# A seven-product up projection in half of a layer's feed-forward part (fp32 split in two, one core)

## Chip, core and metric

One core of a Trainium2 chip runs the whole layer in one launch. The metric is the device time of one execution in microseconds (us); the kernel before has a median of 679.17 us over three runs (679.04 to 679.43).

## The reference

One decoder layer for 512 tokens of width 1024 in fp32: an attention part (a gated delta rule on four heads and block attention on four), a feed-forward part and a gated embedding. The change touches the feed-forward part alone:

```
u2 = rms_norm(h, mlp_pre_norm)                       # 512 x 1024
f  = square(relu(u2 @ w_up)) @ w_down                # w_up 1024 x 4096, w_down 4096 x 1024
h  = h + rms_norm(f, mlp_post_norm)
h  = h + sigmoid(h @ w_ple_gate) * (p @ w_ple)
```

## The kernel before

Every large matmul is done in fp32 by three passes: each operand is split into a high part (a cast to fp32r, on ScalarE) and a low part (the rest, a subtraction on VectorE), and `mm3` (L194) multiplies high by high, high by low and low by high. So each operand tile costs one cast and one subtraction, in `split` (L773) or written out at L958 and L959.

The hidden width 4096 is 32 blocks of 128 columns. Blocks q and q + 16 form pair q; the 16 pairs stand in five groups of 3, 4, 4, 4 and 1 (`GROUPS`, L809). The output of a pair is a tile of `F`, two sides of 512 tokens each. `up` (L881) computes one side: it loads a block of w_up (512 KB), splits it, and runs 8 x 3 matmuls of 512 columns against the normalised, transposed input `u2T`, which is kept split; then ScalarE takes relu and, after the second side, the square. The first four blocks (`EARLY`) run in halves of 256 columns while the attention part ends.

The down projection of the first four groups already goes by seven products in place of eight (the Winograd form of Strassen's): the group's part of f and of w_down are each cut in quarters, and `product` (L950) splits one sum of f quarters and one sum of w_down quarters (`t_op`, L986, on VectorE, in place in raw buffers), multiplies them on TensorE into one of two double banks, `a` or `b`, and adds the bank to one of four sums, C11, C12, C21, C22. Products run in the order 1, 5, 6, 3, 7, 2, 4, with the up projection of the next group's blocks between them (`behind`, L948; `next_up`, L933). The sums lie in SBUF: most products are copied by ScalarE to one of two stage buffers (L981) and added by an accumulating DMA on POOL's queue (L982); in the first group some are copied straight (L972), and those of `ON_V` are added by VectorE (L976).

The last pair (15) is done without the seven products: 16 calls of `mm3`, one for each tile of tokens, half of the width and row block (L1048 to L1057), each pair of calls into a fresh bank that VectorE then adds to the sum (L1056). Then come the norm (POOL and VectorE), transposes on TensorE and the gate (L1069 on).

Buffers of 128x1024 come from two lists, `sf` (raw fp32: 12, of which four hold the sums, two the stages and one a sum of f) and `sr` (split: 15), first in, first out. The order of the instructions on each engine is made by a list scheduler when the kernel is built: what is ready goes in the order of the program. Each engine then runs its own order strictly, and so does each queue of DMA issues (SP for loads, POOL for accumulating DMAs). A split waits for the last matmul that read its buffers.

Of the kernel before, what the change touches and what calls it, by code (L numbers as in the profile page):

```python
# [9 lines left out]
F32 = mybir.dt.float32  # L10
# [5 lines left out]
P = 128  # L16
T = 512
# [53 lines left out]
def hybrid_layer(ctx: ExitStack, tc: tile.TileContext, x, p, w_in, w_tok, w_out, w_up, w_down, w_ple, w_gate,  # L71
# [694 lines left out]
    def norm_r(ss, name):  # L766
# [15 lines left out]
    def halves(pair):
# [78 lines left out]


    NS = NG - 1

    ON_V = {0: (3, 7, 2), NS - 1: (2, 4)}
# [6 lines left out]
    sf.more(F_RIGHT, dn)  # L872
    sr.more(R_RIGHT, dn)
    F = [None, dn.tile([P, PAIRS, 2, T], F32, name="f1")]
    phD = ExitStack()
# [1 line left out]
    F[0] = dd.tile([P, PAIRS, 2, T], F32, name="f0")  # L877
    raw_d = [dd.tile([P, D], F32, name=f"wd{i}") for i in range(8)]
    f_hl = {}

    def up(b, c0, c1, between=None):  # L881
# [17 lines left out]
        if g == NS:  # L899

            if not side:
                f_hl[qi] = [sr.take().rearrange("p (s c) -> p s c", s=2) for _ in range(2)]
            hi, lo = (s[:, side] for s in f_hl[qi])
            nc.scalar.activation(fq[:, side], fq[:, side], AF.Square)
            nc.scalar.copy(hi, fq[:, side])
            nc.vector.tensor_sub(lo, fq[:, side], hi.bitcast(F32))
        elif side:
            nc.scalar.activation(fq[:, :, c0:c1], fq[:, :, c0:c1], AF.Square)

    parts = []  # L910
    for i, b in enumerate(EARLY):
# [10 lines left out]
    S_s = take()  # L922

    stage = [take() for _ in range(2)]
    S = S_s.rearrange("p (j c) -> p j c", j=PAIRS)
    add, sub = nc.vector.tensor_add, nc.vector.tensor_sub

    ups = [b for q in range(HB) for b in (q, q + HB) if b not in EARLY]
    if GROUPS[0] > 2:
        up(ups.pop(0), 0, T)  # L930
        up(ups.pop(0), 0, T)

    def next_up():  # L933
        if ups:
            up(ups.pop(0), 0, T)

    for g in range(NS):
        n, q0 = GROUPS[g], FROM[g]
        f = F[(g + 1) % 2]
        A = {(r, c): f[:, :n, c, 256 * r:256 * r + 256] for r in range(2) for c in range(2)}  # L940
        B = {}
        for i, (r, c, kk) in enumerate((r, c, kk) for r, c in ((0, 0), (0, 1), (1, 1), (1, 0)) for kk in range((n + 1) // 2)):
            B[r, c, kk] = load_rows2(raw_d[i], w_down[:, hf(c)], HB * r + q0 + 2 * kk, min(2, n - 2 * kk))
        banks = {}
        Sn = S[:, :n]

        todo = 2 * GROUPS[g + 1]
        behind = {8: (1, 1, 1, 1, 1, 1, 2), 4: (1, 0, 1, 0, 1, 1, 0), 2: (1, 0, 0, 0, 1, 0, 0)}[todo]  # L948

        def product(i, a, b, bank, c):  # L950

            name, new = bank
            fs = [sr.take(), sr.take()]
            f4 = [s.rearrange("p (j c) -> p j c", j=PAIRS)[:, :n] for s in fs]
            step = 1 if i == 1 else n
            for q in range(0, n, step):
                s = slice(q, q + step)
                nc.scalar.copy(f4[0][:, s], a[:, s])  # L958
                nc.vector.tensor_sub(f4[1][:, s], a[:, s], f4[0][:, s].bitcast(F32))  # L959
            parts = [split(B[b + (kk,)], 512 * min(2, n - 2 * kk)) for kk in range((n + 1) // 2)]  # L960
            w = [x_ for p_ in parts for x_ in halves(p_)]
            if new:
                banks[name] = [(ptr if name == "a" else plv)(f"pd{g}_{i}_{j}") for j in range(2)]
            pts = banks[name]
            for k in range(n):
                for j in range(2):
                    mm3(pts[j], (f4[0][:, k, tk(j)], f4[1][:, k, tk(j)]), w[k], new and k == 0, k == n - 1,
                        go_on=not new)
            sr.give(*fs, *(s for p_ in parts for s in p_))
            if g == 0 and i in (1, 5, 6, 4):  # L970
                for j in range(2):
                    nc.scalar.copy(two(C[c])[:, j], pts[j])  # L972
            elif i in ON_V.get(g, ()):
                for j in range(2):
                    dst = two(C[c])[:, j]
                    add(dst, dst, pts[j])  # L976
# [32 lines left out]
    sf.free = sf.free + [late[i] for i in (8, 9, 6, 7)]  # L1009

    sr.free = [late[i] for i in (10, 11, *range(LATE_F[0]))] + sr.free


    def load_split(src, k0, nk=2):
        s = take()
        got = split(load_rows2(s, src, k0, nk), nk * 512)
        give(s)
        return got
    wd, wd_s = {}, []
    for c in range(2):  # L1020
        for r in range(2):
            s, hl = take(), sr.take()
            load_rows2(s, w_down[:, hf(c)], HB * r + FROM[NS], 1)
            wd[r, c] = hl[:, 0:512], hl[:, 512:D]
            nc.scalar.copy(hl[:, 0:512], s[:, 0:512])
            sub(hl[:, 512:D], s[:, 0:512], hl[:, 0:512].bitcast(F32))
            give(s)
            wd_s.append(hl)
    give(S_s)
# [3 lines left out]
    done = [[two(C[10 * (t // 2) + 11 + i])[:, t % 2] for i in range(2)] for t in range(NT)]  # L1033
    h2T = split_big("h2T")
    h_in = [take() for t in range(NT)]
    for t in range(NT):
# [32 lines left out]
    for i in range(2):  # L1069
# [5 lines left out]
        for t in range(NT):  # L1075
            for c0, c1 in ((0, 512),) if (i, t) != (1, NT - 1) else ((0, 256), (256, 512)):
# [5 lines left out]
                pt = pany(f"pg{i}_{t}_{c0}")  # L1082
# [54 lines left out]
```

## Time and profile before

| | |
|---|---|
| median of three runs | 679.17 us |
| the profiled execution | 679.35 us, of which the span from the first to the last instruction is 677.6 |
| TensorE matmul | 670.6 us busy, 99% |
| VectorE | 442.1 us, 65% |
| ScalarE | 346.4 us, 51% |
| POOL | 54.5 us, 8% |
| matmuls | 3400 |

The feed-forward part runs from about 293 us (first up matmul) to about 625 us (last down matmul). A matmul's row shows its start and a modelled end that overlaps the next one; what one costs in a stream is the distance from start to start.

### The profile page before, as it was taken

To read this page: it belongs to the slowest core of one execution; us is meant where nothing else is said; L and a number is where in the kernel's file an instruction comes from. 1 tells how busy PE (TensorE), PEld (TensorE's weight loads), DVE (VectorE), ACT (ScalarE), POOL (GpSimd) and SP (SyncE) were. 2 spreads that over 40 slices of the span, in tenths; PEclk is the share of its full clock that TensorE was granted. 3 is DMA by queue.
4 is the path that set the end of the run, shared out by engine and by line. 5 is a ranking of instruction groups with operands and counts; after the bars stand their busy time and mean duration, and the time that the engine had idled before them with its cause. 6 is when DMAs were issued, how large, how long until landed. Compare 5 with 4: busy or idle time off the path is not lost.

```text
span 677.6 us, 9102 instructions
## 1 busy us (share of the span) xinstructions
PE 670.6 (99%) x3400; PEld 560.8 (83%) x3400; DVE 442.1 (65%) x703; ACT 346.4 (51%) x648; POOL 54.5 (8%) x91
## 2 busy tenths in 40 slices
PE   9999999999999999999999999999999999999997
PEld 6998888888877778899888888888888888888876
DVE  5759989366776655766664679355774366878752
ACT  6645443532566655555465455655555545773421
POOL 1301100000001100110000001010001010111100
PEclk9999999999999999999999999999999999999999
DMA  8832323532111127575035404675265742394231
GB/s 330 321 126 63 105 90 106 116 119 87 32 32 63 31 64 266 199 255 182 32 111 169 156 31 118 193 194 148 62 167 174 201 96 46 69 277 167 89 130 47
DMA packets 40780, 89.20 MB, mean 132 GB/s; under 512 B 10080, under 2 KB 10720, under 8 KB 40736
## 3 DMA queue, kind: packets, MB, share of 16 engines
q1 hardware_dynamic: 37424, 77.60, 34.2%
q0 software_dynamic: 2736, 9.96, 8.2%
q10 hardware_dynamic: 576, 1.05, 0.5%
q8 instruction: 27, 0.44, 0.3%
q14 instruction: 17, 0.14, 0.1%
HBM read 70.51 MB, written 7.08 MB: 115 GB/s over the span
## 4 chain that ended last, share of the span: by engine, by line
PE 94%; DVE 2%; issue 1%; ACT 1%; DMA 1%; POOL 1%; POOLq 0%; DVEq 0%; ACTq 0%
PE pu L199 17%; PE pd L199 14%; PE pu L196 9%; PE pd L196 7%; PE pc L199 6%; PE po L199 4%; PE pc L196 3%; PE pg L199 3%; PE wv L199 2%; PE po L196 2%; PE pmk L199 2%; PE pmq L199 2%; PE pz L199 2%; PE pav L689 1%; PE pg L196 1%; PE sc L673 1%
## 5 line engine op out<-in xcount | busy, mean ns | idle before, releaser
L199 PE MATMUL pd<-sr,sr 128*128 128x512 f32 x420 | 129.4, 389 | 0.0
L196 PE MATMUL pu<-u2Th,sr 128*128 128x512 f32 (+1 forms) x288 | 105.5, 366 | 0.0
L199 PE MATMUL pu<-u2Th,sr 128*128 128x512 f32 (+1 forms) x288 | 105.3, 366 | 0.0
L199 PE MATMUL pu<-u2Tl,sr 128*128 128x512 f32 (+1 forms) x288 | 105.3, 366 | 0.0
L199 PEld LDWEIGHTS pd<-sr,sr 128*128 128x128 f32 x420 | 78.9, 188 | 16.5
L779 DVE TENSOR_TENSOR sr<-wd,sr 128x1024 fp32r<-128x1024 f32 (+1 forms) x56 | 64.4, 1155 | 42.0 <-PE pu L199 37.3
L196 PE MATMUL pd<-sr,sr 128*128 128x512 f32 x210 | 81.9, 390 | 0.0
L779 DVE TENSOR_TENSOR sr<-sf,sr 128x1024 fp32r<-128x1024 f32 x35 | 42.7, 1223 | 44.9 <-PE pd L199 26.7
L898 ACT ACTIVATE f<-pu 128x512 f32<-128x512 f32 (+1 forms) x36 | 19.8, 551 | 91.7 <-PE pu L199 91.7
L777 ACT CAST sr<-wd 128x1024 fp32r<-128x1024 f32 (+1 forms) x56 | 55.9, 999 | 11.3 <-PE pd L199 9.7
L196 PEld LDWEIGHTS pu<-u2Th,sr 128*128 128x128 f32 x288 | 54.4, 189 | 8.8
L199 PEld LDWEIGHTS pu<-u2Th,sr 128*128 128x128 f32 x288 | 54.3, 189 | 8.7
L199 PEld LDWEIGHTS pu<-u2Tl,sr 128*128 128x128 f32 x288 | 54.4, 189 | 8.7
L196 PEld LDWEIGHTS pd<-sr,sr 128*128 128x128 f32 x210 | 39.4, 188 | 8.3 <-ACT sr L958 0.3
L777 ACT CAST sr<-sf 128x1024 fp32r<-128x1024 f32 x35 | 36.6, 1046 | 10.4 <-DMA sf<-in_w_ple_gate 5.5
L982 POOL DMA_DIRECT2D sf<-sf x19 | 16.7, 878 | 284.7 <-ACT sf L981 279.8
L196 PE MATMUL pc<-uTh,w_h 128*128 128x512 f32 x96 | 38.5, 401 | 0.0
L199 PE MATMUL pc<-uTh,w_l 128*128 128x512 f32 x96 | 38.3, 399 | 0.0
L199 PE MATMUL pc<-uTl,w_h 128*128 128x512 f32 x96 | 38.2, 398 | 0.0
L988 DVE TENSOR_TENSOR wd<-wd,wd 128x1024 f32<-128x1024 f32 (+1 forms) x32 | 36.8, 1156 | 0.7
L981 ACT COPY sf<-pd 128x512 f32<-128x512 f32 x38 | 22.3, 588 | 22.0 <-PE pd L199 21.0
L171 DVE TENSOR_TENSOR w_l<-w_r,w_h 128x1024 fp32r<-128x1024 f32 x12 | 14.7, 1221 | 14.7 <-ACT w_h L170 14.5
(441 smaller groups left out, 1390.3 us busy)
## 6 DMA issues: line engine op xcount, KB each, us to landing
sf<-in_w_up SPq DMA_DIRECT2D x32, 512.0 KB, 3.6
wd<-in_w_down SPq DMA_DIRECT2D x28, 512.0 KB, 5.0
sf<-sf POOLq DMA_DIRECT2D x19, 512.0 KB, 6.6
w_r<-in_w_in SPq DMA_DIRECT2D x12, 512.0 KB, 3.5
wo_r<-in_w_out SPq DMA_DIRECT2D x8, 512.0 KB, 3.7
wv_r<-in_w_tok SPq DMA_DIRECT2D x4, 520.0 KB, 7.1
x<-in_x SPq DMA_DIRECT2D x4, 512.0 KB, 7.0
ple<-pls SPq DMA_DIRECT2D x8, 256.0 KB, 6.6
```

The source lines that it names most:

```text
L171: nc.vector.tensor_sub(lo[:, :n], raw[:, :n], hi[:, :n].bitcast(F32))
L196: nc.tensor.matmul(dst, l[0], r[0], start=start, stop=False, skip_group_check=go_on)
L199: nc.tensor.matmul(dst, a, b, start=False, stop=stop and i == 1, skip_group_check=go_on)
L673: nc.tensor.matmul(sc[:, :N], moq[h][:, tk(i)], mok[h][:, :N], start=True, stop=True)
L689: nc.tensor.matmul(po[:, j * P:], mov[:, j, tk(h)], PT[:, j, j * P:], start=j == 0, stop=j == 3)
L777: nc.scalar.copy(hi[:, :n], src[:, :n])
L779: nc.vector.tensor_sub(lo[:, :n], src[:, :n], hi[:, :n].bitcast(F32))
L898: nc.scalar.activation(fq[:, side, c0:c1], pt[:, :n], AF.Relu)
L981: nc.scalar.copy(two(st)[:, j], pts[j])
L982: nc.gpsimd.dma_start(C[c], st, accum_op=ALU.add)
L988: sub(*(B[i + (kk,)][:, :512 * min(2, n - 2 * kk)] for i in (dst, x_, y_)))
```

## The change

- Pairs 6 to 10 and 12 to 14 (`UP_S`) take the up projection by seven products in place of eight: the contraction (1024) is cut in two, the pair's two sides are the two rows, and the tokens are cut in two halves of 256. Each product is 4 x 3 matmuls of 256 columns. The sums of quarters of `u2T` are made once (`quarter_sums`, during group 0's products) and kept split in eight buffers; the sums of w_up halves are made for each pair.
- The steps of these pairs are laid between the products of the group before by their share of cost (`group_steps`).
- The sums C lie in DRAM. Every product but two goes through a stage buffer and a DMA (plain for the first write, accumulating else); the four sums are loaded back before the tail. In the last of the four groups P2 and P4 stay in their banks, and the last pair's matmuls for the left half of the width go on in them.
- `sf` has 6 buffers in the middle of the feed-forward part (two are stages, four are free for loads), `sr` has 13. The sums of f are made in place in `F`.
- In the tail TensorE follows the order of the program, and VectorE's adds come behind the last split.

```
-F_LEFT, R_LEFT, F_RIGHT, R_RIGHT, R_LATE = 11, 11, 1, 4, 12
-LATE_F = range(6, 10)
+UP_S = (6, 7, 8, 9, 10, 12, 13, 14)
+F_LEFT, R_LEFT, R_RIGHT, R_LATE = 6, 11, 2, 12
+LATE_F = (8, 9, 6, 7, 10, 11)
...
-    C = {i: take() for i in (11, 22, 12, 21)}
+    C = {i: dr.tile([P, D], F32, name=f"sum{i}") for i in (11, 22, 12, 21)}
...
+    t_hl = {i: [k4(s) for s in quarter[2 * n:2 * n + 2]] for n, i in enumerate((1, 3, 2, 4))}
+    Y = {1: quart(0, 0), 2: quart(1, 0), 3: quart(1, 1), 4: t_hl[4], 5: t_hl[1], 6: t_hl[2], 7: t_hl[3]}
+    def quarter_sums():
+        a, b, c = (k4(take()) for _ in range(3))
+        whole = lambda dst, y: add(dst, y[0].bitcast(F32), y[1].bitcast(F32))
+        def parts(i, src):
+            nc.scalar.copy(t_hl[i][0], src)
+            sub(t_hl[i][1], src, t_hl[i][0].bitcast(F32))
+        whole(a, quart(0, 1))
+        whole(b, quart(0, 0))
+        sub(b, a, b)
+        yield
+        whole(c, quart(1, 1))
+        sub(a, c, a)
+        yield
+        sub(c, c, b)
+        parts(1, b)
...
+    def pair_steps(q):
...
+        def mul(dst, x_, y, new):
+            for k in range(HK):
+                mm3(dst, (x_[0][:, k], x_[1][:, k]), (y[0][:, k], y[1][:, k]), new and k == 0, k == HK - 1, go_on=not new)
+        x0, x1 = take(), take()
+        for s, b in ((x0, q), (x1, q + HB)):
+            nc.sync.dma_start(s.rearrange("p (k c) -> p k c", k=KT), w_up[b])
+        p0 = split(x0)
+        a = pmm(f"ua{q}")[:, :HT]
+        mul(a, x_hl(p0, lh), Y[1], True)
+        nc.scalar.copy(fq[:, 0, :HT], a)
+        yield
+        b = pmo(f"ub{q}")[:, :HT]
+        mul(b, x_hl(p0, rh), Y[2], True)
+        add(fq[:, 0, :HT], fq[:, 0, :HT], b)
+        sr.give(*p0)
+        yield
+        s1 = sr.take()
+        add(x1[:, lh], x1[:, lh], x1[:, rh])
+        nc.scalar.copy(s1[:, lh], x1[:, lh])
+        sub(s1[:, rh], x1[:, lh], s1[:, lh].bitcast(F32))
+        sub(x1[:, lh], x1[:, lh], x0[:, lh])
+        p1 = split(x1)
+        mul(a, x_hl(p1, lh), Y[6], False)
+        nc.scalar.copy(fq[:, 0, HT:], a)
+        yield
+        b = pmo(f"uc{q}")[:, :HT]
+        mul(b, [k4(s1[:, s]) for s in (lh, rh)], Y[5], True)
+        nc.scalar.copy(fq[:, 1, HT:], b)
+        sr.give(s1)
+        yield
+        sub(x0[:, lh], x1[:, rh], x1[:, lh])
+        sub(x0[:, rh], x0[:, rh], x1[:, lh])
+        p0 = split(x0)
+        give(x0, x1)
+        mul(a, x_hl(p0, lh), Y[7], False)
+        add(fq[:, 1, HT:], fq[:, 1, HT:], a)
+        yield
+        mul(b, x_hl(p0, rh), Y[3], False)
+        add(fq[:, 0, HT:], fq[:, 0, HT:], b)
+        sr.give(*p0)
+        nc.scalar.activation(fq[:, 0], fq[:, 0], AF.Relu)
+        yield
+        mul(a, x_hl(p1, rh), Y[4], False)
+        nc.scalar.activation(fq[:, 1, :HT], a, AF.Relu)
+        nc.scalar.activation(fq[:, 1, HT:], fq[:, 1, HT:], AF.Relu)
+        sr.give(*p1)
+        squared(q)
+        yield
...
+    def group_steps(g):
+        left = [q for q in range(FROM[g], FROM[g] + GROUPS[g])]
+        cost = [c for q in left for c in ([1.45] * 7 if q in UP_S else [5.45] * 2)]
...
-            if g == 0 and i in (1, 5, 6, 4):
-                for j in range(2):
-                    nc.scalar.copy(two(C[c])[:, j], pts[j])
-            elif i in ON_V.get(g, ()):
...
+            if g == NS - 1 and i in (2, 4):
+                kept[c] = pts
             else:
                 st = stage[0]
                 stage.reverse()
                 for j in range(2):
                     nc.scalar.copy(two(st)[:, j], pts[j])
-                nc.gpsimd.dma_start(C[c], st, accum_op=ALU.add)
-            for _ in range(behind[(1, 5, 6, 3, 7, 2, 4).index(i)]):
-                next_up()
+                if g == 0 and i in (1, 5, 6, 4):
+                    nc.gpsimd.dma_start(C[c], st)
+                else:
+                    nc.gpsimd.dma_start(C[c], st, accum_op=ALU.add)
+            share = min(1, (SEQ.index(i) + 1) / (7 if g < NS - 1 else 6))
+            while did[0] < share - .01:
+                did[0] = next(steps, 1)
+            for _ in range(2 if g == 0 else 0):
+                next(more, None)
...
+    load_back(11, 12, 21)
...
+    load_back(22)
...
+    ctx.enter_context(tc.manual_schedule(engines={mybir.EngineType.PE}))
     for t in range(NT):
         ss = ss_tile(f"qn{t}")
         for i in range(2):
-            pt = pany(f"pd{t}_{i}")
+            pt = p_up(f"pd{t}_{i}") if i else kept[10 * (t // 2) + 11][t % 2]
             for r in range(2):
-                mm3(pt, [s[:, r, tk(t)] for s in f_hl[0]], wd[r, i], r == 0, r == 1)
                 if (t, i, r) == (NT - 1, 0, 0):
                     transpose_done(0)
-            add(done[t][i], done[t][i], pt)
+                mm3(pt, [s[:, r, tk(t)] for s in f_hl[0]], wd[r, i], (i, r) == (1, 0), r == 1, go_on=not i and t > 1)
+            with tc.issue_after(behind["split"].ins):
+                behind["split"] = add(done[t][i], done[t][i], pt)
```

## Rows read from the trace of the kernel before

**Rows 1.** Part 1 of the page, busy us, share of the span and instructions:
```profile
PE 670.6 (99%) x3400; PEld 560.8 (83%) x3400; DVE 442.1 (65%) x703; ACT 346.4 (51%) x648; POOL 54.5 (8%) x91
```

**Rows 2.** Stretches: length; PE, PEld, DVE, ACT, POOL busy; granted clock; DMA share; GB/s:
```profile
380.00:420.00 40.00, 40.00 (x178) 33.12 (x177) 32.19 (x31) 22.63 (x29) 1.55 (x2) 1.00 0.24 67
403.80:485.40 81.60, 81.60 (x361) 67.61 (x360) 49.32 (x45) 44.45 (x59) 6.25 (x7) 1.00 0.56 149
484.00:504.00 20.00, 20.00 (x90) 16.55 (x89) 17.88 (x17) 12.53 (x16) 1.74 (x2) 1.00 0.37 87
```

**Rows 3.** TensorE in order of time, up matmuls (start us, us, engine, instruction):
```profile
293.42 0.28 PE L196 MATMUL pu<-u2Th,sr 128*128 128x256 f32 x1
...
297.61 0.28 PE L199 MATMUL pu<-u2Th,sr 128*128 128x256 f32 x1
...
488.42 0.39 PE L196 MATMUL pu<-u2Th,sr 128*128 128x512 f32 x1
...
491.82 0.39 PE L196 MATMUL pu<-u2Th,sr 128*128 128x512 f32 x1
```

**Rows 4.** VectorE by line and shape, 300 to 660 (busy us, mean ns, idle before):
```profile
L779 DVE TENSOR_TENSOR sr<-wd,sr 128x1024 fp32r<-128x1024 f32 x49 | 59.7, 1222 | 41.7 <-PE pu L199 37.0 <-PE pd L199 4.7
L976 DVE TENSOR_TENSOR sf<-sf,pd 128x512 f32<-128x512 f32 x10 | 6.7, 683 | 14.2 <-PE pd L199 14.2
L959 DVE TENSOR_TENSOR sr<-f,sr 128x256 fp32r<-128x256 f32 x15 | 6.2, 421 | 7.0 <-PE pd L199 6.3 <-ACT sr L958 0.7
L959 DVE TENSOR_TENSOR sr<-sf,sr 128x768 fp32r<-128x768 f32 x4 | 3.8, 952 | 0.0
```

**Rows 5.** VectorE in order of time, queued work of 1024 and of 512 columns:
```profile
408.66 1.22 DVE L994 TENSOR_TENSOR sf<-sf,f 128x1024 f32<-128x1024 f32 x1
409.80 1.22 DVE L779 TENSOR_TENSOR sr<-wd,sr 128x1024 fp32r<-128x1024 f32 x1
...
621.00 0.68 DVE L1056 TENSOR_TENSOR sf<-sf,pd 128x512 f32<-128x512 f32 x1
621.60 0.69 DVE L1061 TENSOR_TENSOR sf<-sf,late 128x512 f32<-128x512 f32 x1
```

**Rows 6.** Waits, 300 to 620 (waiting line, releaser: us, times, longest):
```profile
DVE sr L779 <- PE pu L199: 37.3, 20, 6.2
DVE sr L779 <- PE pd L199: 31.4, 13, 4.3
```

**Rows 7.** ScalarE by line and shape, 300 to 660:
```profile
L777 ACT CAST sr<-wd 128x1024 fp32r<-128x1024 f32 x48 | 50.5, 1052 | 9.2 <-PE pd L199 9.1
L777 ACT CAST sr<-wd 128x512 fp32r<-128x512 f32 x7 | 4.4, 623 | 1.6 <-issue 0.9 <-PE pd L199 0.6
L898 ACT ACTIVATE f<-pu 128x256 f32<-128x256 f32 x7 | 2.7, 387 | 4.7 <-PE pu L199 4.7
```

**Rows 8.** POOL in order of time, the last accumulating DMAs and the norm:
```profile
588.21 0.87 POOL L982 DMA_DIRECT2D sf<-sf  x1 [5.33 <-ACT sf L981]
594.00 0.87 POOL L982 DMA_DIRECT2D sf<-sf  x1 [4.92 <-DMA sf<-sf]
599.14 0.87 POOL L982 DMA_DIRECT2D sf<-sf  x1 [4.26 <-ACT sf L981]
616.75 0.19 POOL L768 TENSOR_SCALAR qn0r<-qn0s 128x1 f32<-128x1 f32 x1 [16.74 <-ACT qn00j L761]
```

**Rows 9.** TensorE in order of time, the tail:
```profile
613.57 0.39 PE L196 MATMUL pd<-late,sr 128*128 128x512 f32 x1
...
645.77 0.50 PE L199 MATMUL pg<-late,h2Tl 128*128 128x512 f32 x1 [0.78 <-DVE h2Tl L211]
```

**Rows 10.** DMA issues (count, KB each, median us to landing):
```profile
sf<-sf POOLq DMA_DIRECT2D x19, 512.0 KB, 6.6
sf<-hd SPq DMA_DIRECT2D x4, 512.0 KB, 4.8
late<-in_norms SPq DMA_DIRECT2D x1, 512.0 KB, 13.5
```

More of the change, by code (lines that the diff above doesn't have):

```diff
@@ L747, in hybrid_layer @@
     sr.more(R_LEFT, m_)
+    phN = ExitStack()
+    n_ = phN.enter_context(tc.tile_pool(name="n", bufs=1, reuse_waits="tile"))
+    sf.more(5, n_)
+    short = sf.free[-5:]
     nw = []
@@ L771, in norm_r @@
         return r
+    behind = {}
     def split(src, n=D, after=None):
@@ L863, in hybrid_layer @@
     NS = NG - 1
-    ON_V = {0: (3, 7, 2), NS - 1: (2, 4)}
+    kept = {}
+    SEQ = (1, 5, 6, 3, 7, 2, 4)
     up_no = [0]
@@ L879, in hybrid_layer, with squared @@
     f_hl = {}
+    def squared(q):
+        g = group_of(q)
+        fq = F[(g + 1) % 2][:, q - FROM[g]]
+        nc.scalar.activation(fq, fq, AF.Square)
+        if g == NS:
+            hi, lo = f_hl[q - FROM[g]] = [sr.take().rearrange("p (s c) -> p s c", s=2) for _ in range(2)]
+            nc.scalar.copy(hi, fq)
+            nc.vector.tensor_sub(lo, fq, hi.bitcast(F32))
     def up(b, c0, c1, between=None):
@@ L898, in up @@
         nc.scalar.activation(fq[:, side, c0:c1], pt[:, :n], AF.Relu)
[L899 to L908, printed above, removed]
+        if side and c1 == T:
+            squared(q)
     parts = []
@@ L918, in hybrid_layer @@
     give(*xrs)
-    C = {i: take() for i in (11, 22, 12, 21)}
+    C = {i: dr.tile([P, D], F32, name=f"sum{i}") for i in (11, 22, 12, 21)}
     two = lambda s: s.rearrange("p (j c) -> p j c", j=2)
-    S_s = take()
+    assert all(any(l is f for f in sf.free) for l in short)
+    sf.free = [f for f in sf.free if all(f is not l for l in short)]
+    phN.close()
+    q_ = ctx.enter_context(tc.tile_pool(name="q", bufs=1, reuse_waits="tile"))
+    quarter = [(q_ if i < 5 else dn).tile([P, D], F32R, name=f"uq{i}") for i in range(8)]
@@ new lines, in hybrid_layer @@
+    t_hl = {i: [k4(s) for s in quarter[2 * n:2 * n + 2]] for n, i in enumerate((1, 3, 2, 4))}
[16 more added lines that the diff above has]
+        yield
+        whole(b, quart(1, 0))
+        parts(2, c)
+        yield
+        sub(b, b, c)
+        parts(3, a)
+        yield
+        parts(4, b)
+        give(*(t.rearrange("p k c -> p (k c)") for t in (a, b, c)))
+        yield
@@ new lines, in plain_steps @@
+    def plain_steps(q):
+        for b in (q, q + HB):
+            if b not in EARLY:
+                up(b, 0, T)
+                yield
+    def group_steps(g):
+        left = [q for q in range(FROM[g], FROM[g] + GROUPS[g])]
+        cost = [c for q in left for c in ([1.45] * 7 if q in UP_S else [5.45] * 2)]
+        run = 0
+        for c, _ in zip(cost, (None for q in left for _ in (pair_steps if q in UP_S else plain_steps)(q))):
+            run += c
+            yield run / sum(cost)
+    for q in range(2, GROUPS[0]):
+        for _ in plain_steps(q):
+            pass
@@ L937, in hybrid_layer @@
+    more = quarter_sums()
     for g in range(NS):
@@ L966, in product @@
                 for j in range(2):
-                    mm3(pts[j], (f4[0][:, k, tk(j)], f4[1][:, k, tk(j)]), w[k], new and k == 0, k == n - 1,
+                    mm3(pts[j], (f4[0][:, k, tk(j)], f4[1][:, k, tk(j)]), w[k], new and k == 0,
+                        k == n - 1 and (g, i) not in ((NS - 1, 2), (NS - 1, 4)),
                         go_on=not new)
             sr.give(*fs, *(s for p_ in parts for s in p_))
-            if g == 0 and i in (1, 5, 6, 4):
-                for j in range(2):
-                    nc.scalar.copy(two(C[c])[:, j], pts[j])
-            elif i in ON_V.get(g, ()):
-                for j in range(2):
-                    dst = two(C[c])[:, j]
-                    add(dst, dst, pts[j])
+            if g == NS - 1 and i in (2, 4):
+                kept[c] = pts
             else:
@@ L1008, in hybrid_layer @@
     late = [dr_.tile([P, D], F32 if i in LATE_F else F32R, name=f"late{i}") for i in range(R_LATE)]
-    sf.free = sf.free + [late[i] for i in (8, 9, 6, 7)]
-    sr.free = [late[i] for i in (10, 11, *range(LATE_F[0]))] + sr.free
+    sf.free = sf.free + [late[i] for i in LATE_F]
+    sr.free = quarter[5:] + [late[i] for i in range(6)] + sr.free + quarter[:5]
     def load_split(src, k0, nk=2):
@@ L1018, in load_split, with load_back @@
         return got
+    back = {}
+    def load_back(*quarters):
+        for c in quarters:
+            back[c] = take()
+            nc.gpsimd.dma_start(back[c], C[c])
+    load_back(11, 12, 21)
     wd, wd_s = {}, []
     for c in range(2):
+        s = take()
         for r in range(2):
-            s, hl = take(), sr.take()
-            load_rows2(s, w_down[:, hf(c)], HB * r + FROM[NS], 1)
+            hl, raw = sr.take(), s[:, hf(r)]
+            nc.sync.dma_start(raw, w_down[tk((HB * r + FROM[NS])), hf(c)])
             wd[r, c] = hl[:, 0:512], hl[:, 512:D]
-            nc.scalar.copy(hl[:, 0:512], s[:, 0:512])
-            sub(hl[:, 512:D], s[:, 0:512], hl[:, 0:512].bitcast(F32))
-            give(s)
+            nc.scalar.copy(hl[:, 0:512], raw)
+            sub(hl[:, 512:D], raw, hl[:, 0:512].bitcast(F32))
             wd_s.append(hl)
-    give(S_s)
+        give(s)
     gate_w = lambda i: [x_ for k0 in range(0, KT, 2) for x_ in halves(load_split(w_gate[:, hf(i)], k0))]
@@ L1032, in hybrid_layer @@
     load_norm(3)
-    done = [[two(C[10 * (t // 2) + 11 + i])[:, t % 2] for i in range(2)] for t in range(NT)]
+    load_back(22)
+    done = [[two(back[10 * (t // 2) + 11 + i])[:, t % 2] for i in range(2)] for t in range(NT)]
     h2T = split_big("h2T")
```

61 lines of the change are left out of this document (33 added, 28 removed).

## The prediction

> **What bounds the kernel now.** I read part 1 of the page first: TensorE is busy 670.6 of 677.6 us [rows 1]. By stages it is busy without a gap from one end of the feed-forward part to the other, at a granted clock of 1.00, while VectorE has 49.3 of 81.6 us in one whole group of four pairs (group 1's products with the up projection of pairs 7 to 10) and ScalarE 44.5 [rows 2]. The reader sees that one engine sets the time and that only fewer or shorter matmuls, or a new gap, can move it. VectorE's own waits say the same: in the 320 us of the feed-forward part its subtractions in `split` wait 37.3 us for up matmuls and 31.4 us for down matmuls, that is for split buffers to come free, not for anything slower [rows 6].
>
> **The sum on TensorE.** 16 matmuls 512 columns wide start 3.40 us apart from first to last, so 0.2267 us each; 36 of 256 columns, in the same program lines with the same operands, take 4.19 us from first to last, so 0.1197 us each [rows 3]. A plain pair is 2 blocks x 24 = 48 wide matmuls, 10.88 us. A pair by seven products is 7 x 4 x 3 = 84 narrow ones, 10.05 us. So one pair gives 0.83 us, and eight give 6.6 us. A narrow matmul costs 0.53 of a wide one, which takes back 0.53 us of the eighth (1.36 us) that seven products for eight promise. Nothing else on TensorE changes in number: the last pair still has 48 wide matmuls, half of them now added to banks that hold P2 and P4.
>
> The Trainium skill ("TensorE: Matmul & The Clock Gate", section "Back-to-back issue gap") gives N/2.4 + 2.5 ns for an isolated gap, 215.8 and 109.2 ns. By that a pair would give 1.19 us and the eight 9.5 us, and with the stalls taken below the time would be 671.3. The rows are some 11 ns longer at either width, and they are of this very form, so they decide.
>
> **VectorE, the price.** A 128x1024 subtraction lasts 1.22 us, 512 columns 0.685, 256 columns 0.42 [rows 4]. Two that queue start 1.14 us (1024) and 0.60 us (512) apart [rows 5]. I keep both as ends, and 0.42 for 256. A plain pair needs two of 1024: 2.3 to 2.4 us. A pair by seven products needs three of 1024 (the splits of x0, x1 and x0 again), five of 512 (one for s1's low part, four sums and differences of the weight halves) and three adds of 256 out of PSUM: 7.7 to 8.35 us. The products of a group of four need 21 subtractions in splits (the first of f in four quarters), 8 for `t_op` and 4 for the sums of f: 38.2 to 40.7 us. By stretches:
> - group 1's products with pairs 7 to 10, all by seven: 68.9 to 74.1 us of VectorE in 168 x 0.2267 + 336 x 0.1197 = 78.3 us of TensorE, 88 to 95%;
> - group 2's with pairs 11 (plain), 12, 13, 14: 63.5 to 68.2 in 79.2, 80 to 86%;
> - group 0's with pairs 3 to 5 plain, pair 6 and the quarters (8 sums and 4 splits of 1024, 14.6 us): at most 62.0 in 71.3 (768 columns at 0.95 [rows 4]), 87%.
> Six 512-wide adds of group 0 and the four after P2 and P4 at the end go. ScalarE per new pair: three casts of 1.05 us, one of 0.62, three copies of 0.39 out of PSUM, 1.4 of relu, a square of 1.05 like a cast [rows 7]: 7.4 us against 4.4, which makes 60 of 78.3 us in the fullest stretch, 77%. It is not the bound.
>
> **Is VectorE's work hidden?** TensorE needs it in time as well as in sum. There are 13 split buffers in place of 15, taken in turn. Counting them through the new order, the six of a product come free when the product before it ends; the four up steps between the two (48 x 0.1197 = 5.75 us) are all the cover for its three splits (3.4 to 3.7 us), and the buffers of the up steps come free 9.8 to 12.6 us ahead. One turn is 5.44 + 5.75 = 11.2 us. In the turn ahead of P3 of group 1 VectorE has two sums of f, two `t_op`, three splits, and of pair 8 one add, the work on x1 and the new x0: 13.7 to 14.8 us, 2.5 to 3.6 too much. The turn ahead of P6 needs 11.2 to 12.0, that ahead of P5 10.2 to 11.0; the turns after P3 have about 5 us over. So the backlog is 1.5 us (2.5 less the 1.0 saved up) at queueing prices and 4.4 at the single ones. Against it: the last two steps of pair 8 (2.9 us of TensorE) wait for no new split and may be put into the gap, below nothing it cannot go. Bounds 0 to 4.4; I take 0.8, half of the queueing price, since the rows show these subtractions queueing in just such a burst. Group 2 has less to do in the same place, and group 0's quarters are ready long ahead of use; both at 0, bounds 0 to 2.
>
> **Handovers.** Three times in a pair a bank is added to again after ScalarE or VectorE has read it, with one step of 1.44 us between. A narrow matmul ends 0.16 us after its turn (0.28 less 0.12 [rows 3]); a copy of 0.39 behind one running cast of 1.05 is done at 1.60, an add of 0.42 behind one running subtraction of 1.22 at 1.80. So each costs 0 to 0.36 us when one instruction is ahead, and on an idle engine nothing: 24 handovers, 0 to 8.6, of which I take 0.8 (most find the engine less than half way from free, and the order is made with them in view). What queues behind a late add is the next subtraction of a split, and behind that the next product.
>
> **The rest.** Group 0's sums go through a stage buffer and a DMA in place of ScalarE copies and VectorE adds into SBUF: a turn there is 9.5 us, and the stages alternate, so the DMA's 6.6 us [rows 10] is covered twice over. DRAM as its target is not in the trace; nearest is that 6.6 us. In the tail the fourth sum (C22) is the last: P7's DMA is issued at 599.14 [rows 8], so 599.14 + 0.87 + 6.6 = 606.6, then 0.87 to issue the load on the same POOL queue and 4.8 us (the nearest load of DRAM data) to 13.5 us (the slowest load) [rows 10] to land: 612.3 to 621.0. TensorE's last pair starts at 613.57 and its sixth block ends 12 x 0.68 = 8.2 us later, at 621.7 [rows 9]. Covered, barely so at the slow end. POOL's next work behind these loads, the norm, started at 616.75 [rows 8]. POOL already waited 4.92 us there for one sum's DMA to end before the next into the same sum [rows 8]; if DRAM takes longer this grows. The fixed order of TensorE in the tail is nearly that of the trace; the 0.78 us gap there waits for VectorE [rows 9], and I leave it: 0, bounds -0.8 to 1. Loads of w_up now need two raw buffers a pair out of four, which come free some 20 us ahead of use, against 3.6 us for a load: nothing.
>
> **Sum.** The profiled execution took 679.35 us; -6.6 + 0.8 + 0.8 gives 674.35. The runs shown have a median of 679.17, 0.18 lower: **674.2 us**.
>
> **Rivals.**
> 1. All of VectorE's work is covered: the whole 6.6 us stay, 672.6. For it: VectorE kept 17.9 of 20 us, 89%, in a burst without a gap on TensorE [rows 2]. Against: 88 to 95% for 78 us, not for 20.
> 2. VectorE becomes the bound in the group of pairs 7 to 10, then in its neighbours: TensorE waits for each product's splits. It decides where VectorE gets under 74.1 / (78.3 + 6.6) = 87% at single prices. At 84% the three stretches take 88.2, 81.2 and 73.8 us, 14.4 more than TensorE's: 687.0. At the 80% of the busiest 40 us of now [rows 2] they take 26.6 more: 699. At 80% but queueing prices only the first is longer, 86.1, by 7.8: 680.4, no change. For it: cast, subtraction and buffer wait on one another in turn. Against: the 89%, and idle time that now is put down to buffers held by TensorE.
> 3. The sums come back late. If an accumulating DMA into DRAM took twice 6.6 us, P6's, issued at 588.21 [rows 8], would end at 588.2 + 14.1 = 602.3 before P3's into the same sum starts, P7's land at 617.3 and be back at 623 to 632, 1.3 to 10 us late; with 4, 678.2.
>
> **Chances.** Forecast (673.2 to 677.8) 0.47; rival 1 0.25; rival 2 with loss 0.15, its no-change form 0.08; rival 3 0.05. A measurement here can't tell less than about 0.2% (1.4 us) from no change. Faster 0.72, same 0.13, slower 0.15. Range 672.3 to 681: below it 0.06, above it 0.13.
>
> **What would show it.** 864 narrow and 288 wide up matmuls (192 and 672 now), TensorE's busy time near 664 us, VectorE's near 490. In the stretch of pairs 7 to 10 the gaps on TensorE should be near 2 us, most ahead of a `pd` of P3. Gaps spread over every product, with VectorE as releaser and without idle time itself, are rival 2; a gap at the last pair behind a DMA is rival 3. A pitch of narrow matmuls far from 0.12 us would break the sum itself.

## The result and the profile after

The changed kernel takes 673.23 us (median of six runs, 672.40 to 673.68) against 679.11 for the kernel before: a ratio of 0.9912, 95% interval 0.9899 to 0.9925. 674.2 was forecast, faster. The profiled execution took 673.41 us with a span of 671.6. Part 1 of its page, which answers to [rows 1]:

```profile
PE 664.3 (99%) x3688; PEld 567.9 (85%) x3688; DVE 488.7 (73%) x776; ACT 375.8 (56%) x702; POOL 60.5 (9%) x102
```

TensorE is 6.3 us less busy and stands still 0.3 us longer (671.6 - 664.3 = 7.3, against 7.0): together the 6.0 us of the span. Of the 6.3, 0.4 lies ahead of the first up matmul, where the change does nothing. VectorE's 488.7 and TensorE's 664.3 are the 490 and 664 of the forecast. The stretch of [rows 2] once more, then group 1's products by themselves, and the work around P3 of group 1 in steps of 20 us (PE, PEld, DVE, ACT, POOL busy; granted clock; DMA share; GB/s):

```profile
403.80:485.40 81.60, 81.31 (x517) 73.80 (x517) 70.53 (x81) 58.61 (x87) 5.93 (x7) 1.00 0.64 162
...
400.20:479.10 78.90, 78.61 (x506) 71.56 (x505) 68.76 (x81) 55.91 (x83) 5.93 (x7) 1.00 0.62 154
...
395.00:415.00 20.00, 20.00 (x135) 18.42 (x133) 19.97 (x23) 14.79 (x22) 1.41 (x2) 1.00 0.38 102
415.00:435.00 20.00, 20.00 (x135) 18.53 (x134) 20.00 (x24) 15.12 (x22) 1.70 (x2) 1.00 0.51 107
...
455.00:475.00 20.00, 20.00 (x126) 17.95 (x125) 12.78 (x18) 13.59 (x21) 1.23 (x2) 1.00 0.67 180
```

VectorE went from 49.3 to 70.5 us of the 81.6, or 86%. In group 1's products it has 68.8 of 78.9 us, where 68.9 to 74.1 of 78.3 were forecast. For 40 us, 395 to 435, it has next to no idle time (0.03 us): this is the burst that the prediction counted ahead of P3. Yet TensorE has no gap there. Its one wait on record in the feed-forward part is at 477.58. The first fence is TensorE, the second VectorE at the same place, in order of time:

```profile
477.01 0.28 PE L200 MATMUL uc<-u2Th,sr 128*128 128x256 f32 x1
477.58 0.39 PE L197 MATMUL ua<-uq,sr 128*128 128x256 f32 x1 [0.28 <-DVE f L1019]
```

```profile
475.97 1.22 DVE L786 TENSOR_TENSOR sr<-wd,sr 128x1024 fp32r<-128x1024 f32 x1
477.11 0.41 DVE L1019 TENSOR_TENSOR f<-f,ua 128x256 f32<-128x256 f32 x1
477.44 1.22 DVE L786 TENSOR_TENSOR sr<-sf,sr 128x1024 fp32r<-128x1024 f32 x1
```

The last step is a handover as it was worked out: the add that reads bank `ua` stands behind one running subtraction of 1.22 us, and `ua` is added to again 0.57 us after the last `uc` matmul in place of 0.12. So 0.45 us is lost where the record names 0.28, since matmul ends are modelled. But VectorE is not full there: between 455 and 475 it is busy 12.8 of 20 us. What stands ahead of its last steps is a load of w_down. ScalarE's cast waits 2.65 us for that load, and VectorE 4.22 us for the cast (ScalarE, then VectorE in the changed kernel; the third is ScalarE's row in E8 below, a run whose code is the same up to the last group's products):

```profile
471.23 1.05 ACT L784 CAST sr<-wd 128x1024 fp32r<-128x1024 f32 x1 [2.65 <-DMA wd<-in_w_down]
```

```profile
472.31 1.22 DVE L786 TENSOR_TENSOR sr<-wd,sr 128x1024 fp32r<-128x1024 f32 x1 [4.22 <-ACT sr L784]
```

```profile
471.10 1.05 ACT L784 CAST sr<-wd 128x1024 fp32r<-128x1024 f32 x1 [1.89 <-DMA wd<-in_w_down]
```

The load took 5.5 us from issue to landing here and 4.7 in E8, where TensorE loses nothing at this place. Over five profiles with this step the loss goes with ScalarE's wait: 1.89 us and none (E8), 2.58 and 0.34 (E11), 2.65 and 0.45 (here), 3.08 and 0.57 (E5), 3.47 and 0.57 (E7). No run takes the load away, and why its time varies was not settled.

VectorE's waits between 300 and 620 us shifted against [rows 6]: on up matmuls 6.4 us where it was 37.3, on down matmuls 7.0 where it was 31.4, 21.1 on ScalarE's casts, and 7.6 on loads of w_up (waiting line, releaser: us, times, longest):

```profile
DVE sr L786 <- ACT sr L784: 21.1, 14, 4.2
DVE sf L1001 <- DMA sf<-in_w_up: 7.6, 5, 2.5
DVE sr L786 <- PE pd L200: 7.0, 6, 1.7
...
DVE sr L786 <- PE pu L200: 6.4, 4, 1.7
```

Three stretches of one execution are told apart by two starts on TensorE: the first up matmul and the first one of the last pair (613.57 in [rows 9]). The table gives what lies before, between and behind, to the end of the span, in us; E1 to E12 are the runs below (not E7 and E9, whose last pair does not begin at one clear row).

| kernel | before first up | feed-forward | tail |
|---|---|---|---|
| before | 293.4 | 320.15 | 64.0 |
| after | 293.0 | 314.58 | 64.0 |
| after, second profile (E11) | 293.5 | 314.76 | 67.1 |
| E1, no pair by seven | 293.7 | 320.20 | 63.2 |
| E2, eight plain pairs in halves | 293.6 | 325.56 | 63.6 |
| ten pairs (E3, E12) | 293.1, 293.7 | 313.08, 313.64 | 63.1, 63.0 |
| E4, twelve pairs | 293.2 | 313.45 | 63.0 |
| E10, eleven pairs | 293.9 | 314.26 | 64.7 |
| E5, one split dearer | 293.3 | 315.00 | 63.9 |
| E6, three splits dearer | 293.3 | 319.17 | 63.9 |
| E8, P2 and P4 not kept in banks | 293.6 | 314.10 | 79.1 |

The change acts in the middle column alone: -5.57 us. Ahead of it, where these kernels are alike, their profiles differ by up to 0.9 us, the two of the changed kernel by 0.5; in the tail those two differ by 3.

### The profile page after: what moved, and what is told of

Read it like the earlier page. It is cut to its first block, busy times and chain, and to the rows that moved or that the text cites. A ratio compares the mean times of both kernels' runs of the same rounds, so it can differ in the third digit from the quotient of the medians.

```text
span 671.6 us, 9864 instructions
## 1 busy us (share of the span) xinstructions
PE 664.3 (99%) x3688; PEld 567.9 (85%) x3688; DVE 488.7 (73%) x776; ACT 375.8 (56%) x702; POOL 60.5 (9%) x102
## 3 DMA queue, kind: packets, MB, share of 16 engines
q0 software_dynamic: 4320, 15.73, 12.8%
## 4 chain that ended last, share of the span: by engine, by line
PE 94%; DVE 2%; ACT 1%; issue 1%; DMA 1%; POOL 0%; POOLq 0%; ACTq 0%; DVEq 0%
PE pd L200 15%; PE pu L200 9%; PE pd L197 8%; PE pc L200 7%; PE ua L200 5%; PE pu L197 4%; PE po L200 4%; PE pc L197 3%; PE pg L200 3%; PE ua L197 2%; PE wv L200 2%; PE po L197 2%; PE pmk L200 2%; PE pmq L200 2%; PE uc L200 2%; PE pz L200 2%
## 5 line engine op out<-in xcount | busy, mean ns | idle before, releaser
L197 PE MATMUL pu<-u2Th,sr 128*128 128x512 f32 (+1 forms) x160 | 55.6, 348 | 0.0
L200 PE MATMUL pu<-u2Tl,sr 128*128 128x512 f32 (+1 forms) x160 | 55.5, 347 | 0.0
L200 PE MATMUL pu<-u2Th,sr 128*128 128x512 f32 (+1 forms) x160 | 55.4, 347 | 0.0
L786 DVE TENSOR_TENSOR sr<-sf,sr 128x1024 fp32r<-128x1024 f32 x40 | 48.7, 1221 | 4.3 <-ACT sr L784 3.0
L784 ACT CAST sr<-sf 128x1024 fp32r<-128x1024 f32 x40 | 42.1, 1054 | 5.3 <-DVE sf L1004 3.6
L1076 DVE TENSOR_TENSOR sr<-f,sr 128x1024 fp32r<-128x1024 f32 (+2 forms) x39 | 33.4, 873 | 9.8 <-PE pd L200 6.7
L1095 ACT COPY sf<-pd 128x512 f32<-128x512 f32 x52 | 30.1, 587 | 14.4 <-PE pd L200 13.1
L1075 ACT CAST sr<-f 128x1024 fp32r<-128x1024 f32 (+2 forms) x39 | 29.6, 776 | 13.6 <-DVE f L1116 8.0
L1099 POOL DMA_DIRECT2D sum<-sf x22 | 18.7, 851 | 195.2 <-ACT sf L1095 187.5
L200 PE MATMUL ua<-uq,sr 128*128 128x256 f32 x192 | 35.1, 281 | 0.0
L197 PEld LDWEIGHTS pu<-u2Th,sr 128*128 128x128 f32 x160 | 30.3, 189 | 3.8
L200 PEld LDWEIGHTS pu<-u2Th,sr 128*128 128x128 f32 x160 | 30.3, 189 | 3.8
```

The source lines that it names most:

```text
L197: nc.tensor.matmul(dst, l[0], r[0], start=start, stop=False, skip_group_check=go_on)
L200: nc.tensor.matmul(dst, a, b, start=False, stop=stop and i == 1, skip_group_check=go_on)
L786: behind["split"] = nc.vector.tensor_sub(lo[:, :n], src[:, :n], hi[:, :n].bitcast(F32))
```

## The experiments

Theory: the whole gain is TensorE's, 84 narrow matmuls for 48 wide ones in each of eight pairs, and VectorE's added work is hidden as long as splits run ahead of the matmuls. First rival: the gain is in the other edits (sums, banks, order). Second rival: VectorE is the bound and has already eaten part of the gain.

**E1: no pair by seven products, all else of the change kept**

```
-UP_S = (6, 7, 8, 9, 10, 12, 13, 14)
+UP_S = ()
```

> All pairs plain; the rest of the change stays (sums in DRAM, P2 and P4 kept in banks, fixed TensorE order in the tail, 13 split buffers, the quarter sums still made and then not used). Theory (the gain is TensorE's columns, the rest is worth nothing): 8 x 0.83 = 6.6 us above the changed kernel, 0.3 of its gaps gone: 679.5, like the kernel before. Rival A (part of the gain is the tail's or the sums'): below 678.4. Rival B (the rest costs and the seven products give more than counted): above 680.5.

678.40 us, 0.9993 of the kernel before (0.9984 to 1.0002). The other edits together are worth nothing that can be told: 678.40 is 1.1 us under the theory's 679.5 and at the border of rival A, but the feed-forward part has its old length, 320.20, and the tail (63.2 against 64.0) differs by less than it does between two profiles of one kernel. The gain in the feed-forward part is that of the eight pairs: 5.62 us in the table, and 5.2 of the 5.9 by medians.

**E2: the eight pairs plain, but in two halves of 256 columns**

```
+                if q in UP_H:
+                    up(b, 0, HT)
+                    yield
+                    up(b, HT, T)
```

> As all pairs plain, but the eight pairs run their two blocks in two halves of 256 columns each: 96 narrow matmuls in place of 48 wide ones, same products, no seven. Theory (a narrow matmul costs 0.1197 us against 0.1133 for half a wide one): 8 x (11.49 - 10.88) = 4.9 us above the all-plain kernel, 684.4. Rival (only the 2.5 ns a matmul of the Trainium skill's page 'TensorE: Matmul & The Clock Gate', section 'Back-to-back issue gap', is lost by narrow ones): 8 x 0.12 = 1.0 us above it, 680.5.

683.85 us, 1.0074 (1.0061 to 1.0086); TensorE's busy time by part 1 of the pages of E1 and E2:

```profile
PE 670.7 (99%) x3400; PEld 560.8 (83%) x3400; DVE 449.7 (66%) x704; ACT 353.8 (52%) x654; POOL 60.5 (9%) x102
```

```profile
PE 676.1 (99%) x3784; PEld 580.8 (85%) x3784; DVE 448.9 (66%) x704; ACT 356.6 (52%) x670; POOL 60.5 (9%) x102
```

The same arithmetic in 768 narrow matmuls for 384 wide ones costs 5.4 us. With the table's 5.36 that is (384 x 0.2267 + 5.36) / 768 = 0.1203 us for each narrow one, all told, where the prediction had 0.1197 [rows 3]. At that price eight pairs give 8 x (10.88 - 84 x 0.1203) = 6.2 us, not 6.6. Yet the pitch of the narrow matmuls is not what grew. One step of 48 in E2 and the wide matmuls behind it, TensorE in order of time:

```profile
469.52 0.28 PE L198 MATMUL pu<-u2Th,sr 128*128 128x256 f32 x1
...
475.28 0.40 PE L198 MATMUL pd<-sr,sr 128*128 128x512 f32 x1
```

The 48 take 5.76 us to the start of the next; all 768 take 92.05 us from start to start, 0.1199 each, which is 5.0 us more than the 384 wide ones. The other 0.35 us is in the 612 down matmuls between 340 us and the last pair (139.13 us, against 138.78 in E1): the first two wide ones behind a narrow step start 0.233 and 0.236 us apart in place of 0.227.

**E3 and E12: ten pairs by seven products; E11: the changed kernel again, on one chip with E12**

```
-UP_S = (6, 7, 8, 9, 10, 12, 13, 14)
+UP_S = tuple(range(5, 15))
```

> Pairs 5 to 14 by seven products, ten in place of eight (5 and 11 added). Theory (TensorE's columns alone count, VectorE's work is still covered): 2 x 0.83 = 1.7 us below the changed kernel, 671.6, gaps on TensorE under 1 us. Rival (VectorE is at its limit: 96% of group 0's stretch, 88 to 95% of group 2's): the gaps eat the gain or more, 673 to 677, with gaps on TensorE released by VectorE.

> The changed kernel itself, once more, beside the next run on one chip: 673.2 us +-0.5, ratio to the kernel before 0.990 to 0.9925.

> Ten pairs by seven products (pairs 5 to 14), once more, on one chip with the changed kernel: if the two additional pairs are worth what was seen across calls (about 1.1 us of the 1.66 that two pairs' columns come to), 672.1 us, 0.7 to 1.5 below the changed kernel of this call. Rival: that difference was the spread of the runs; then the two are within 0.3 us.

E3 672.09 us, 0.9899 (0.9886 to 0.9913). E12 671.80, 0.9893 (0.9880 to 0.9905), beside E11's 674.01, 0.9929 (0.9911 to 0.9947). Ten pairs are the best version of this study, 1.1 us below the changed kernel's first runs and 2.2 below E11 on one chip. E11 is 0.3 us above its expected range, and so the 2.2 lies outside the 0.7 to 1.5 expected of E12. The feed-forward part gives 0.9 to 1.7 of it by the two profiles of each kernel, for the 1.5 us that two more pairs are worth at E2's price; the rest is the tail, told below.

**E4: twelve pairs, the quarter sums ahead of all products; E10: eleven pairs, with the last one**

```
-UP_S = (6, 7, 8, 9, 10, 12, 13, 14)
+UP_S = tuple(range(3, 15))
+    for _ in more:
+        pass
```

```
+UP_S = tuple(range(5, 16))
```

> Pairs 3 to 14 by seven products, twelve; the quarter sums are all made ahead of group 0's products. Theory (columns alone): 4 x 0.83 = 3.3 us below the changed kernel, 669.9. Rival (VectorE at its limit): group 0's stretch holds 65.1 us of VectorE in 68.8 of TensorE at single prices and the quarters (14.6 us) fall into the up work ahead of it, so 3 to 8 us of gaps on TensorE before and in group 0's products, 673 to 678.

> Pairs 5 to 15 by seven products, eleven. Against the kernel with pairs 5 to 14: theory (columns) 0.83 us less, 671.3. Rival (VectorE is at its end in group 3's stretch, where the tail's splits are made too, and the last square comes late): no gain or up to 2 us more, 672 to 674.

E4 672.16 us, 0.9900 (0.9886 to 0.9913); E10 673.44, 0.9912 (0.9900 to 0.9925). Neither beats ten. E4 lies between its theory (669.9) and its rival (673 to 678), E10 in its rival's range. In E4's feed-forward part TensorE is busy 312.1 us, where E3 and E12 have 313.0 and 313.4, so most of the 1.5 us of two pairs came off; but it stands 1.4 us there where they stand 0.1 and 0.3, for 1.0 us of it near 396, for ScalarE's copy of a bank. E10 has five waits of 0.2 to 0.5 us, and its busy time is 664.4, more than the 662.7 and 663.8 of ten pairs. A part of each wait shows as busy time, as at 477.58: counted from start to start, E10 loses 2.0 to 2.6 us more than ten pairs do between the first up and the last down matmul, where one more pair gives 0.8.

**E5 and E6: the low part of one split (E5) or of three (E6) per new pair written twice**

```
+        sub(p1[1], x1, p1[0].bitcast(F32))
```

> The changed kernel with one more VectorE subtraction of 1024 columns in each of the eight pairs (the low part of x1's split written twice with the same values). In the stretch of pairs 7 to 10 VectorE's demand goes from 68.9 to 73.5 us at queueing prices, 74.1 to 79.0 at single prices, in 78.3 us of TensorE. Theory (queueing prices hold in a full queue, so there is room): 673.2 to 674.2, gaps on TensorE under 1.5 us. Rival (single prices hold, VectorE is at its end already): the stretch is over-full, 675 to 679.

> The changed kernel with three more VectorE subtractions of 1024 columns in each of the eight pairs (the low part of all three splits written twice with the same values). In the stretch of pairs 7 to 10 VectorE's demand is 82.6 us at queueing prices and 88.7 at single prices in 78.3 us of TensorE; in that of pairs 11 to 14 it is 73.8 and 79.2 in 79.2. Theory (queueing prices): 4 to 6 us of gaps, nearly all in the first of these stretches, 677.5 to 679.5. Rival (single prices): 10 to 13 us in both, 683.5 to 687. If nothing moves (under 674.5), VectorE's work is not what limits this kernel at all.

E5 674.02 us, 0.9919 (0.9907 to 0.9931); E6 677.39, 0.9978 (0.9967 to 0.9990). Eight subtractions more cost 0.8 us against the changed kernel's first runs and nothing against E11's 674.01; 24 cost 4.2. By the queueing price of 1.14 us that is 9.1 and 27.4 us of VectorE: the first is hidden nearly whole, of the second a sixth shows. By the expectation's sum at single prices E6 would have cost 10 to 13. In E6 VectorE is busy 77.26 of 80 us between 400 and 480, 97%. TensorE in E6 in order of time, and the stretch around it (PE busy, clock, DMA share, GB/s):

```profile
436.36 0.56 PE L200 MATMUL ua<-uq,sr 128*128 128x256 f32 x1 [1.41 <-DVE sr L1019]
...
439.07 0.41 PE L200 MATMUL uc<-u2Tl,sr 128*128 128x256 f32 x1
439.28 0.41 PE L200 MATMUL uc<-u2Th,sr 128*128 128x256 f32 x1
```

```profile
430.00:435.00 5.00, 4.64 (x35) 1.00 0.68 104
435.00:440.00 5.00, 3.64 (x17) 0.66 0.65 223
```

The up step that stands 1.41 us waits for its own doubled subtraction (L1019), which is behind 40 us of VectorE without idle time; the split of f for P3 is the next in VectorE's queue. I read this as the burst ahead of P3 grown until it shows. But a part of the gap is the run's own doing: the matmul waits for the doubled write, which ends at 436.31, while the first write of the same values ended at 434.04, before the step began. A run with as many subtractions on a buffer that nothing waits for was not made. The gap is paid twice: after it the narrow matmuls start 0.21 us apart for 3.3 us (granted clock 0.66 over the 5 us, so at the lower level, 1.2 GHz, for most of them), which costs another 1.5 us.

**E9: 11 split buffers in place of 13**

```
-F_LEFT, R_LEFT, R_RIGHT, R_LATE = 6, 11, 2, 12
+F_LEFT, R_LEFT, R_RIGHT, R_LATE = 6, 11, 0, 12
```

> The changed kernel with 11 split buffers in place of 13. A pair and a product between its steps hold up to 11 at once, so splits lose their lead over TensorE. Theory (what hides VectorE's 88% is the lead that the buffers give): 2 us or more of new gaps on TensorE, in the stretch of pairs 7 to 10 first, 675 to 680. Rival (the order alone hides it, the buffers are ample): 673.2 to 673.8.

677.64 us, 0.9992 (0.9978 to 1.0006): 4.4 us of the gain are gone, though VectorE's work is the same. TensorE's two longest waits in E9, in order of time:

```profile
480.03 0.38 PE L197 MATMUL ua<-uq,sr 128*128 128x256 f32 x1 [1.51 <-DVE f L1019]
...
600.54 0.51 PE L197 MATMUL pd<-sr,sr 128*128 128x512 f32 x1 [0.49 <-ACT sr L784]
```

With two buffers less the same add of `ua` comes 1.5 us late, and again VectorE had stood idle before it, for a load (VectorE in E9):

```profile
472.14 0.69 DVE L1001 TENSOR_TENSOR sf<-sf 128x512 f32<-128x512 f32 x1 [4.13 <-DMA sf<-in_w_up]
```

This load was issued at 464.97, in the changed kernel at 458.53. So it is the lead, of splits and of the loads that follow on them, and not the share of busy time that hides VectorE; that fewer split buffers are why this load is issued late is argued, not shown by itself.

**E7: TensorE's tail without the written order**

```
-    ctx.enter_context(tc.manual_schedule(engines={mybir.EngineType.PE}))
```

> The changed kernel without the written order of TensorE's tail (the last pair's products, transposes and gate products may be taken in any order). My theory: the tail's edits are worth nothing to within a microsecond; the changed kernel has one wait of 0.64 us there, for the first gate product's transposed operand, and the kernel before had one of 0.78 us at the same place, so that neither order is clearly better: 673.2 us +-0.6, ratio to the kernel before 0.9905 to 0.992. Rival A: the written order is what keeps the down products of the last pair behind their sums without a hole; free, TensorE stands 1 to 3 us in the tail: 674.2 to 676. Rival B: the written order costs the 0.64 us; free, 672.5 and no wait in the tail.

674.21 us, 0.9922 (0.9909 to 0.9935), which is at the edge of rival A's range; but the changed kernel on the same chip (E11) has 674.01: no difference. The gaps move to other gate products (two waits of 0.6 us for a split of gate weights).

**E8: P2 and P4 of the last group through stage and DRAM like the others**

```
-            if g == NS - 1 and i in (2, 4):
-                kept[c] = pts
-            else:
+            if True:
...
-            pt = p_up(f"pd{t}_{i}") if i else kept[10 * (t // 2) + 11][t % 2]
+            pt = p_up(f"pd{t}_{i}")
```

> The changed kernel with P2 and P4 of the last group put through a stage tile and the accumulating transfer like the other products, and the last pair's down products in banks of their own that are added afterwards. My theory: the sums that P2 and P4 feed come back only after two more accumulating transfers on POOL's queue. In the changed kernel's trace such transfers stood 7.4 to 8.2 us one behind the other (582.18, 590.76, 599.50), and the last load took 7.36 us; P4's bank is done near 607, so its transfer is done near 617 and the load near 624. The first addition of the tail (VectorE) is then held until about 624 in place of about 610, and the banks of the last pair wait behind it; the gate products (near 640 in the changed kernel) have some 15 us of other TensorE work ahead of them. Estimate: 0 to 10 us of TensorE's idle in the tail, 5 taken: 678 us. Rival: the tail's work covers it all: 673.2 +-0.6. Rival: four additions more on VectorE and the sums' way are serial: over 685.

687.76 us, 1.0129 (1.0116 to 1.0142). The rival's size came out, not mine. POOL's queue in E8 in order of time, and TensorE's first wait behind it:

```profile
608.62 0.89 POOL L1096 DMA_DIRECT2D sum<-sf  x1
616.14 0.56 POOL L1142 DMA_DIRECT2D sf<-sum  x1 [6.63 <-DMA sum<-sf]
616.68 0.89 POOL L1096 DMA_DIRECT2D sum<-sf  x1
624.76 0.56 POOL L1142 DMA_DIRECT2D sf<-sum  x1 [7.18 <-DMA sum<-sf]
```

```profile
622.82 0.80 PE L197 MATMUL pd<-uq,sr 128*128 128x512 f32 x1 [9.51 <-DVE sf L1187]
```

The first sum back is loaded at 616.14, the addition that frees a bank starts at 622.07, and TensorE has no other work that may go first. Two waits of 9.5 and 2.1 us make 11.6; TensorE's busy time is 4.4 us longer than the changed kernel's (668.7 against 664.3) for the same matmuls, and the clock behind the first wait is low (the stretches after it; PE busy, clock, DMA share, GB/s):

```profile
620.00:625.00 5.00, 2.19 (x5) 0.50 0.69 156
625.00:630.00 5.00, 5.00 (x21) 0.71 0.44 157
```

11.6 + 4.4 - 0.64 (the changed kernel's own tail gap) = 15.4, for 15.2 in the spans. So the sums in DRAM cost nothing only together with the last pair's matmuls added in the banks; E1 measures the two edits together.

## Why the prediction was right

**Columns.** Right, the pitch included. The 864 narrow and 288 wide up matmuls are there. In E8, where no up matmul waits, the 672 new narrow ones take 80.43 us from start to start, 0.1197 each, as forecast; in the changed kernel's profile 80.89, the same with the 0.45 us of its one wait. What the sum had at nothing is the step from narrow to wide matmuls: the 612 down matmuls told under E2 take 139.17 us in the changed kernel, 138.78 in E1. So 6.6 us was forecast and 6.2 is left at E2's price. The Trainium skill ("TensorE: Matmul & The Clock Gate", section "Back-to-back issue gap") with 109.2 and 215.8 ns would make E2 1.0 us dearer than E1; 5.4 was measured, so the rows were the right source.

**Backlog ahead of P3.** The burst was there, but cost nothing where 0.8 was taken. VectorE in the changed kernel, the last two splits of P3, and TensorE's first matmul of P3:

```profile
430.76 1.23 DVE L1076 TENSOR_TENSOR sr<-f,sr 128x1024 fp32r<-128x1024 f32 x1
431.89 1.23 DVE L786 TENSOR_TENSOR sr<-wd,sr 128x1024 fp32r<-128x1024 f32 x1
```

```profile
433.68 0.39 PE L197 MATMUL pd<-sr,sr 128*128 128x512 f32 x1
```

The last split ends at 433.12, 0.56 us ahead of the matmul. The prediction allowed VectorE 1.0 us of work saved up from earlier turns; it worked without a pause from 394.43 and so was 0.56 us early in place of 1.5 us late. The lower bound, 0, was the value, and its margin half a microsecond: E6, with three subtractions more in each pair, loses 1.7 us just ahead of P3, a part of it by its doubled write.

**Price of VectorE's operations.** The prediction kept 1.14 (queued) and 1.22 (single) as ends. The rows decide for the first: the two splits above start 1.13 us apart, and the 68.8 us of group 1's products are the 68.9 of queueing prices. E5 and E6 fit that. Rival 2 put the limit at 84% or 80%; VectorE ran at 86% for 82 us with 0.45 us lost, and at 97% in E6 with some 4 us lost. Both its forms fall. Two pairs more still pay (E3, E12), four don't (E4); that VectorE is why is not shown, since the longest wait of E4 is for ScalarE.

**Handovers.** 0.8 taken for 24, 0.45 found, at one place. Its last step is the one worked out, a bank's reader behind one running subtraction, and the longest waits of E4 and of E9 are also for a bank's reader. But by the profiles it was a load that made the reader late here, and the same handover costs nothing in E8. So the size is near by luck.

**Loads.** Put at nothing, with buffers free "some 20 us ahead of use"; only loads of w_up were counted. That step was wrong: VectorE waited for loads of w_up five times (7.6 us), and the one gap on TensorE comes behind a load of w_down. It cost half a microsecond in the changed kernel and none in E8.

**Sums through DRAM and the tail.** Taken at nothing, and so found in the middle column (E1: +0.05 us). Rival 3 was half right: accumulations into one sum behind each other took longer than the 6.6 us assumed (they start 8.58 and 8.74 us apart, more than the 7.4 to 8.2 named ahead of E8). POOL in the changed kernel, answering to [rows 8]:

```profile
582.18 0.84 POOL L1099 DMA_DIRECT2D sum<-sf  x1 [4.62 <-ACT sf L1095]
590.76 0.85 POOL L1099 DMA_DIRECT2D sum<-sf  x1 [7.73 <-DMA sum<-sf]
598.95 0.56 POOL L1145 DMA_DIRECT2D sf<-sum  x1 [7.34 <-DMA sum<-sf]
599.50 0.89 POOL L1099 DMA_DIRECT2D sum<-sf  x1
607.75 0.56 POOL L1145 DMA_DIRECT2D sf<-sum  x1 [7.36 <-DMA sum<-sf]
```

From issue to the next step took 7.3 to 7.7 us behind the issue's 0.85. C22's load is issued at 607.75 and lands 7.6 us later, at 615.4, where the prediction had 4.8 to 13.5 us. The block that is added to it is done 8.2 us after the last pair's start at 607.55, at 615.7: covered by 0.3 us. VectorE comes to that add only behind 620.78, so nothing waits for the load.

**Cancelled errors.** Forecast were -6.6 for columns and +1.6 for stalls, -5.0. In the feed-forward part -5.57 was found: the columns as forecast, 0.45 lost behind the load, and some 0.6 in small pieces, 0.4 of it in the down matmuls, most of that behind narrow steps. So about 1.0 was lost where 1.6 was taken, and not by the two terms taken: the backlog cost nothing, and the handover came behind a load. The mechanism and its main term were right; that the stall terms came near what other things cost is luck. The other 0.4 us of the 6.0 in the span lies ahead of the first up matmul, inside what the profiles differ by there.

## What to carry to other kernels

Price an exchange of wide matmuls for narrow ones by running the same work in halves: here a narrow one, all told 6% dearer than half a wide one (0.1203 against 0.1133 us), took 0.6 of the 1.4 us that seven products for eight promise. An engine may stand at 86% of a stretch, and without idle time for 40 us, and not be the bound if its results run ahead by some buffers; count the buffers before calling it full. Where the bound engine waits for it all the same, look whether the late engine had itself stood idle before: here it had, for a load. Where a result goes by way of DRAM, look for the one consumer with nothing else to do, and keep that last piece on the chip.

## What was not expected of the hardware

Two profiles of the changed kernel differ by 3.8 us of span (671.6 and 675.4), 3.1 of it in the tail. The chain of waits in both (start, us, what) runs through one load of gate weights, the cast and subtraction of its split, and the transposed operand's low part, which stands behind that subtraction on VectorE (its high part stands behind that cast on ScalarE). The changed kernel's first profile, then E11:

```profile
631.46 5.23 DMA late<-in_w_ple_gate
636.71 1.06 ACT sr L784
637.79 1.23 DVE sr L786
639.02 0.61 DVE h2Tl L212
639.67 0.50 PE pg L200
```

```profile
632.17 6.80 DMA late<-in_w_ple_gate
639.00 1.05 ACT sr L784
640.07 1.23 DVE sr L786
641.30 0.61 DVE h2Tl L212
641.96 0.80 PE pg L200
```

The same 512 KB took 5.23 us and 6.80 us. The longer one left waits of 1.37 and 0.64 us, and behind them the clock fell, which cost some 1.6 us by the starts of eight matmuls (E11; PE busy, clock, DMA share, GB/s):

```profile
640.00:645.00 5.00, 3.78 (x9) 0.67 0.81 268
```

With ten pairs the load came in time in both profiles (no wait on TensorE in the tail). Why it varies was not settled; that the tail's spread is this load and the clock behind it is read from two profiles, not tested by a run that takes the load away. It is the same kind of thing as the wait at 477.58: a load that lands 0.8 or 1.6 us later, where the engines behind it have no more lead than that.
